# Latent attention on one core: its opening, four head-pair lists and the work between them written as one sequence

## The chip, the cores and the metric

The kernel runs on one core of one Trainium2 chip. A core has a matrix engine (TensorE, PE in the profile), three engines for elementwise work (VectorE or DVE, ScalarE or ACT, GpSimd or POOL), a queue engine (SyncE or SP) that mostly starts DMAs, and 16 DMA engines. [...] The metric is the device time in microseconds (us) of one execution: 1699.26 us before the change, the median of 3 runs (1699.22 to 1700.66).

## What is computed

One layer of a hybrid encoder step, on 1024 prompt tokens and 32 sample tokens with a cache of 512. All of it is float32; a product is formed from three matmuls over high and low parts of both operands. The change concerns branch A, the multi-head latent attention of the prompt (8 heads, taken in four pairs), and what is computed beside it.

```python
p = h @ w_in
q_lat, c_kv, k_r, q_b, k_b, v_b, g_a, g_b = jnp.split(p, IN_SPLITS, axis=-1)
q = (rms_norm(q_lat, g_q_lat) @ w_uq).reshape(B, T, H_A, NOPE + ROPE)
k_nope, v_a = expand_latent(c_kv, w_uk, w_uv)
s = (jnp.einsum('bqhd,bshd->bhqs', q_nope, k_nope)
     + jnp.einsum('bqhr,bsr->bhqs', q_rope, k_rope)).astype(jnp.float32) * MLA_SCALE
mask = (kpos[None, :] // CHUNK) <= (qpos[:, None] // CHUNK)
p = jax.nn.softmax(jnp.where(mask, s, NEG), axis=-1)
o_a = jnp.einsum('bhqs,bshd->bqhd', p.astype(v.dtype), v)
merged = g_a * (o_a @ w_proj_a) + g_b * (o_b @ w_proj_b)
```

## The kernel before

The stages run one after the other: input norm, combined projection, stick-breaking attention (branch B), latent vectors (`stage_lat`), latent attention (`stage_mla`), merge, ConvFFN. `stage_mla` is the one that changes.

Its heads go in four pairs p = 0 to 3. For each pair a *list* of tokens is written out by hand. A token names a pair, an action and a tile of the score matrix, and every token issues its instructions at once; inside a `manual_schedule` block TensorE, ScalarE and VectorE get them in exactly that order. SP and POOL (the DMAs) are not in the block; they go as soon as their queue and semaphores let them. The actions:

- `S` scores of a 128-row block (three matmuls of 256 to 512 columns and a mask of 64), `M`, `n`, `m` the negative maximum (VectorE), `E` the exponential with its sum (ScalarE), `s`, `R` sum and reciprocal, `C` or `c` the division (VectorE or ScalarE).
- `T` turn the probabilities (TensorE), `h` and `v` split them into high (ScalarE) and low (VectorE), `V` multiply by the value rows, `o` and `p` gather the two halves of the result.
- fill of the same list: `D` starts the next pair's expansion, `I` and `i` split its weights, `x` queries, `y` keys, `z` and `B` rotary parts, `X` and `K` query evacuation, `J` and `j` query splits, `H`, `g`, `L`, `b` key splits, `Z` the sample's queries, `Y` steps of the sample's own attention, `N` and `k` loads.
- fill shared by all: the output projection of branch B (`proj_b`). `U` loads weights, `W` and `w` split them, `f` is one step of three 264-column matmuls, `G` evacuates and stores a block. Its moving operand comes from DRAM in two halves of four tiles and is split into `ObH` (ScalarE) and `ObL` (VectorE).

Before the change there are three written orders. The *opening* is one string that expands pair 0, `zzzBBzzzBBzzzBByyHgLbyyHgLbxxxXKxxxXKxxxXK`, followed by the value blocks (`values`, four blocks of 12 matmuls, each followed by two evacuations on ScalarE and two on VectorE), the query splits, the rotary key rows, the first four operands (`O`), the store of the rotated keys (`krope_out`) and the first weight split. `ORDER_M` holds lists 0 and 1, `ORDER_N` lists 2 and 3. Between the two stand, in no written order, the sample's latent transposes (`mla_sample_latents`), the value blocks of the second half of the heads, the second half of the operands and four weight steps. Where one block ends and the next begins, the framework merges their instructions by its own estimate.

The lists overlap: list 1 begins while list 0 still turns its last probabilities. PSUM has eight banks: two each of the tags `mm` and `tr`, three of `s`, one of `pv`. The value rows of lists 2 and 3 take the two buffers of lists 0 and 1 (tag `V`), weights come through two buffers (`wr`), and of tag `big`, which holds query tiles and the operands' second half, there are three.

Lines in the profile are often a helper's: L68 is `hi` (a high part on ScalarE), L71 `lo` (a low part on VectorE), L75 to L77 the three matmuls of `mm3`, L806 the transposes of `T`, L820 the matmuls of `V`, L1615 to L1620 those of `S`, L954 to L959 the maxima, L961 the exponential, L1552 the value evacuation, L1830 the load of an operand, L1877 and L1878 `G`.

Of the kernel before, what the change touches and what calls it, by code (L numbers as in the profile page):

```python
# [17 lines left out]
P = 128  # L18
# [26 lines left out]
class K:  # L45
# [777 lines left out]
    def sb_weights(self, pieces, w):  # L823
# [27 lines left out]
        0S0.1 0M0.1 0n0.1 0S1.1 0E0.1 0S0.0 f4 W f 0M0.0 0n0.0 G 0M1.1 0n1.1 f2 w 0R0.1 0E1.1 f 0S1.0 0C0.1  # L851
        0M1.0 0E0.0 0S2.0b f2 0S2.0a f G 0R1.1 0n1.0 0R0.0 0M2.0b 0c0.0 0E1.0 0T0.0 0C1.1 0M2.0a 0h0.0 0m2.0 f
        0E2.0a 0R1.0 f2 0D 0c1.0 0S2.1b 0v0.0 G 0M2.1b 0S2.1a 0M2.1a 0m2.1 f 0E2.0b 0V0.0 0E2.1a f 0S3.0b 0M3.0b
        f 0o0 0E2.1b 0T1.1 0S3.0a 0p0 0T1.0 0s2.1 f G 0h1.1 0S3.1a 0M3.0a 0h1.0 0R2.1 0m3.0 f 0v1.1 0C2.1 f
        0s2.0 0M3.1a 0E3.0b f2 0S3.1b 0E3.0a G 0R2.0 0v1.0 f2 0c2.0 0M3.1b 0V1.1 0I 0V1.0 0S4.0b 0m3.1 0T2.1
        0E3.1a 0T2.2 0h2.2 0S4.0a 0i G 0M4.0b 0z 0M4.0a 0o1 0z 0m4.0 0E3.1b 0s3.0 0E4.0a 0v2.2 0z 0z 0z 0R3.0
        0s3.1 0T2.0 0h2.1 0B 0S4.1b 0h2.0 0B 0p1 0S4.1a 0V2.2 0E4.0b 0c3.0 0v2.1 0R3.1 W 0C3.1 0v2.0 0V2.1 0z
        0T3.2 0s4.0 0h3.2 0z 0M4.1a 0S5.0b 0M4.1b 0T3.3 0m4.1 0z 0E4.1b 0B 0M5.0b 0h3.3 0B 0V2.0 0S5.0a 0v3.3
        0o2 0M5.0a 0z 0B 0E4.1a 0m5.0 0x 0T3.1 0s4.1 0x 0B 0p2 0x 0R4.1 0v3.2 0S5.1b 0X 0V3.3 0E5.0b 0h3.1 0V3.2
        0v3.1 0E5.0a 0T3.0 0R4.0 0C4.1 0V3.1 0K 0h3.0 0c4.0 0v3.0 U 0S5.1a 0x 0M5.1b 0S6.1 0V3.0 0T4.3 0x 0o3 0x  # L860
        0M5.1a 0x 0s5.0 0m5.1 0T4.2 0h4.3 w 0M6.1 0v4.3 0x 0E5.1b 0X 0K 0p3 0h4.2 0R5.0 0T4.1 0h4.1 0n6.1 0x U
        0v4.2 0E5.1a 0E6.1 0V4.3 0s5.1 0c5.0 0X 0K 0V4.2 0T4.0 0S6.0 0v4.1 0R5.1 0h4.0 f 0C5.1 0J 0v4.0 f 0M6.0
        0S7.0 0n6.0 f 0V4.1 0T5.1 0T5.2 0M7.0 0V4.0 f 0h5.1 0j 0h5.2 G 0y 0v5.2 f 0E6.0 0R6.1 0y 0n7.0 0o4 f
        0R6.0 0H f 0E7.0 f 0T5.0 0p4 0C6.1 0c6.0 0L 0S7.1 0h5.0 0v5.1 0M7.1 0v5.0 0V5.2 0g 1S1.1 W 0T6.1 G 0n7.1
        0V5.1 0h6.1 0R7.0 1M1.1 0b 1n1.1 0E7.1 0V5.0 0y 0o5 0T6.0 1E1.1 0c7.0 0v6.1 0h6.0 1S0.0 0p5 w 0y 1S1.0
        1M0.0 f 0R7.1 0C7.1 0g 0V6.1 f 0H f 0T7.0 1S0.1 0v6.0 0V6.0 W 1n0.0 f 0b 1E0.0 1S2.0b 1M1.0 0L 1R0.0
        1n1.0 f w 1M0.1 1n0.1 1c0.0 0h7.0 1M2.0b 1E1.0 0o6 f 0v7.0 0p6 1S2.0a 1E0.1 1M2.0a f 1R0.1 f 1R1.0 1m2.0
        0J 1C0.1 1S2.1b 0V7.0 G G 0j 1R1.1 f 1M2.1b f 1T0.0 0o7 1E2.0b f 1C1.1 1S2.1a 1D U 1M2.1a 1E2.0a 1S3.0a
        1m2.1 f2 1c1.0 1h0.0 W 0p7 f 1s2.0 1E2.1a 1T1.0 1E2.1b 1M3.0a 1S3.0b 1S3.1b 1v0.0 w 1M3.0b G 1V0.0 1m3.0
        1s2.1 1R2.0 1T1.1 1h1.0 1o0 f 1R2.1 f 1E3.0a 1h1.1 G f 1M3.1b 1p0 1S3.1a 1E3.0b f 1c2.0 1v1.0 1k f 1v1.1  # L870
        1M3.1a 1s3.0 1m3.1 1C2.1 1V1.1 1V1.0 1S4.0a 1T2.2 f 1E3.1a 1o1 1E3.1b 1p1 1S4.0b 1T2.1 1M4.0a f 1h2.2
        1s3.1 G 1R3.0 1R3.1 f 1v2.2 1h2.1 1c3.0 1S4.1b 1M4.0b f 1v2.1 1T2.0 1m4.0 1C3.1 1V2.2 f 1E4.0a 1h2.0
        1S4.1a 1T3.3 1M4.1b 0Z 1v2.0 1I 1V2.1 1V2.0 1M4.1a 1E4.0b 1m4.1 1h3.3 1v3.3 1E4.1b 1o2 1i 1s4.0 1T3.2
        1E4.1a 1S5.0a 1S5.0b 1T3.1 1x 1h3.2 1S5.1b 1p2 1R4.0 1M5.0b G 1s4.1 1R4.1 1N 1c4.0 1x 1V3.3 1M5.0a 1m5.0
# [12 lines left out]
        f 0n1.0 0h0.0 0E1.0 0s2.0 0v0.0 0M2.1b 0R1.0 0M2.1a 0m2.1 0c1.0 0V0.0 0C1.1 G 0S3.0a 0M3.0a f2 0E2.1b
        0E2.1a 0T1.0 0S3.0b 0o0 0T1.1 f 0s2.1 0M3.0b 0h1.1 f 0m3.0 0R2.1 0R2.0 0p0 f 0h1.0 0E3.0b 0v1.1 0S3.1a f
        0S3.1b 0C2.1 f 0M3.1a 0c2.0 0M3.1b 0v1.0 0E3.0a f 0s3.0 G 0T2.0 0h2.0 0m3.1 0S4.0a 0E3.1a 0E3.1b 0v2.0 G
        f 0V1.1 0S4.0b 0T2.2 0M4.0a 0h2.2 f 0V1.0 0M4.0b 0T2.1 0m4.0 0o1 0h2.1 f 0p1 0s3.1 f 0S4.1a 0R3.0 f G  # L890
        0R3.1 0E4.0b f 0C3.1 0v2.1 0E4.0a 0v2.2 0c3.0 0M4.1a 0s4.0 0S5.0a 0S4.1b 0M4.1b f2 0V2.2 0T3.3 0m4.1 0I
        0M5.0a 0E4.1a 0V2.1 0T3.2 0h3.3 0i 0S5.0b 0V2.0 0v3.3 0M5.0b 0h3.2 G 0E4.1b 0x 0m5.0 0x 0v3.2 0T3.1 0o2
        0s4.1 0h3.1 0p2 0S5.1b 0R4.0 0x 0V3.3 U 0R4.1 0V3.2 0E5.0a 0c4.0 0v3.1 0T3.0 0C4.1 0S5.1a 0h3.0 0M5.1b
        0X 0M5.1a 0m5.1 0v3.0 0x 0T4.3 0E5.0b W 0E5.1b 0S6.0 0x 0h4.3 0M6.0 w 0n6.0 0v4.3 0E5.1a 0s5.0 0x 0K
        0V3.1 0V3.0 0T4.2 0X 0x 0s5.1 0R5.0 0T4.1 0o3 0p3 U 0x 0h4.2 0E6.0 0h4.1 0V4.3 0R5.1 0x 0v4.2 0K 0R6.0
        0V4.2 0T4.0 0C5.1 0v4.1 0S7.1 0S6.1 0X 0Z 0K 0h4.0 0c5.0 0V4.1 0T5.2 0Z 0J 0v4.0 f 0h5.2 f 0V4.0 f 0M7.1
        0n7.1 f 0M6.1 0E7.1 0j 0o4 0R7.1 0n6.1 0T5.1 G 0y 0p4 0y 0C7.1 0h5.1 0v5.2 0E6.1 0H 0v5.1 0R6.1 0C6.1
        0T5.0 f 0S7.0 0V5.2 0L 0h5.0 0J 1S0.0 0c6.0 f3 0T6.1 0M7.0 0g 0v5.0 0n7.0 0V5.1 0V5.0 0T6.0 1M0.0 0j 0b
        G 1S0.1 1n0.0 W 0h6.1 0E7.0 w 0R7.0 0o5 f 0c7.0 0v6.1 1M0.1 0y 0y f2 0h6.0 0p5 1n0.1 f 0V6.1 1S1.0 0T7.0
        1E0.1 W 0v6.0 1E0.0 1S2.0b 1S1.1 G 0h7.0 0V6.0 f 0H f2 0g f 1Y 1M1.0 1R0.1 0v7.0 1n1.0 1M1.1 1R0.0 1E1.0  # L900
        1c0.0 0o6 1Y 0L 1C0.1 1n1.1 1S2.0a 1R1.0 0p6 0V7.0 w 1E1.1 G 1Y 1M2.0b 1T0.0 1R1.1 1Y 0o7 1S2.1b f
        1M2.0a 1Y 1m2.0 1h0.0 1E2.0b 1c1.0 0p7 1M2.1b 1C1.1 1E2.0a 1v0.0 U 1S2.1a 1M2.1a 1s2.0 1V0.0 f 1Y 1T1.1
        1o0 1Y 1m2.1 1E2.1b 0b 1p0 1h1.1 1v1.1 1E2.1a 1s2.1 1T1.0 1R2.1 1h1.0 1R2.0 1C2.1 1Y 1V1.1 1v1.0 1c2.0
        1T2.1 1S3.0a 1h2.1 1T2.2 f 1Y 1V1.0 1v2.1 1Y f 1S3.0b 1T2.0 1M3.0a f 1Y f 1M3.0b 1m3.0 1h2.2 1o1 1S3.1a
        1v2.2 W 1q 1p1 1E3.0a 1E3.0b 1S3.1b 1Y 1M3.1a 1S4.0b 1V2.2 G 1M3.1b 1Y 1s3.0 1m3.1 1M4.0b 1Y 1V2.1
        1E3.1b 1Y 1R3.0 1S4.0a 1r 1h2.0 1v2.0 1E3.1a 1Y 1s3.1 1R3.1 1q 1M4.0a w 1C3.1 1c3.0 1Y 1m4.0 1S4.1b
        1T3.3 1E4.0a 1h3.3 1Y 1E4.0b 1M4.1b 1v3.3 1Y 1S4.1a 1V2.0 1T3.1 1Y 1M4.1a 1s4.0 1m4.1 1h3.1 1E4.1a 1o2
        1v3.1 1r 1T3.2 1p2 1Y 1V3.3 1h3.2 1v3.2 1V3.2 1T3.0 1E4.1b f 1V3.1 1s4.1 1R4.0 1R4.1 1c4.0 1h3.0 1S5.0a
        1Y 1Y 1C4.1 1v3.0 1T4.1 1T4.3 f 1M5.0a 1Y 1h4.3 1v4.3 1V3.0 1h4.1 1o3 1S5.1b G 1v4.1 1S5.0b 1T4.2 1M5.0b
        1Y 1m5.0 f 1q f 1p3 1h4.2 1V4.3 1E5.0b 1v4.2 1Y 1V4.2 1E5.0a 1r 1M5.1b 1T4.0 1S5.1a 1Y 1h4.0 1Y 1s5.0  # L910
# [1799 lines left out]
```

## Time and profile before

| | us |
|---|---|
| median of 3 runs | 1699.26 |
| profiled execution | 1700.54 |
| its span, first to last instruction | 1698.8 |
| latent attention, first opening matmul to last list row | about 573 to 840 |

| engine | busy, us | share of the span |
|---|---|---|
| PE (matmul) | 1647.6 | 97% |
| PEld (weight loads) | 1511.4 | 89% |
| DVE | 1269.9 | 75% |
| ACT | 1008.5 | 59% |
| POOL | 300.3 | 18% |

Two kinds of rows need a word. A row of a stretch gives its bounds, its length, and the busy time of PE, PEld, DVE, ACT and POOL in it with the number of instructions in brackets; then the clock that TensorE was granted (1.00 is full), the busy share of the DMA engines and GB/s. A row of the timeline gives start, length, engine, line, operation, tiles out<-in, shape and count, and in square brackets how long the engine sat idle before it and what it waited for. Neighbouring equal instructions are merged into one row. Matmuls overlap, so their lengths add up to more than the time they take; the step from one start to the next is what one of them costs.

### The profile page before, as it was taken

To read this page: it belongs to the slowest core of one execution; us is meant where nothing else is said; L and a number is where in the kernel's file an instruction comes from. 1 tells how busy PE (TensorE), PEld (TensorE's weight loads), DVE (VectorE), ACT (ScalarE), POOL (GpSimd) and SP (SyncE) were. 2 spreads that over 40 slices of the span, in tenths; PEclk is the share of its full clock that TensorE was granted. 3 is DMA by queue.
4 is the path that set the end of the run, shared out by engine and by line. 5 is a ranking of instruction groups with operands and counts; after the bars stand their busy time and mean duration, and the time that the engine had idled before them with its cause. 6 is when DMAs were issued, how large, how long until landed. Compare 5 with 4: busy or idle time off the path is not lost. (4 is left out here: it accounts for less than half of the span.)

```text
span 1698.8 us, 30285 instructions
## 1 busy us (share of the span) xinstructions
PE 1647.6 (97%) x11592; PEld 1511.4 (89%) x11592; DVE 1269.9 (75%) x2140; ACT 1008.5 (59%) x1945; POOL 300.3 (18%) x581
## 2 busy tenths in 40 slices
PE   5999999999999989999899999999999999999997
PEld 2899999999998879888788789999999999877885
DVE  4865698988873678888666789887777877787455
ACT  4544697978874568887763475444444444554442
POOL 5113312111110221111000212211111222200013
PEclk8999999999999989999999999999999999999999
DMA  9336885576532523321373532433333333697643
GB/s 358 103 109 198 277 244 163 164 194 182 169 111 56 163 79 96 96 62 60 110 250 127 181 124 77 150 107 133 127 104 131 131 104 121 240 321 246 205 139 121
DMA packets 194146, 260.62 MB, mean 153 GB/s; under 512 B 23375, under 2 KB 132305, under 8 KB 193937
## 3 DMA queue, kind: packets, MB, share of 16 engines
q1 hardware_dynamic: 172944, 198.50, 37.5%
q0 software_dynamic: 20688, 59.56, 9.9%
q8 instruction: 91, 1.49, 0.4%
q10 hardware_dynamic: 368, 0.63, 0.1%
q14 instruction: 55, 0.44, 0.1%
HBM read 191.11 MB, written 67.82 MB: 152 GB/s over the span
## 5 line engine op out<-in xcount | busy, mean ns | idle before, releaser
L68 ACT ACTIVATE wh<-wr 128x1024 fp32r<-128x1024 f32 (+2 forms) x151 | 130.2, 864 | 228.7 <-PE s L2164 85.8
L71 DVE TENSOR_TENSOR wl<-wr,wh 128x1024 fp32r<-128x1024 f32 (+2 forms) x151 | 148.3, 985 | 79.4 <-ACT wh L68 79.0
L75 PE MATMUL mm<-hh,wh 128*128 128x352 f32 x456 | 152.5, 334 | 0.1
L76 PE MATMUL mm<-hl,wh 128*128 128x352 f32 x456 | 148.5, 326 | 0.1
L77 PE MATMUL mm<-hh,wl 128*128 128x352 f32 x456 | 148.3, 325 | 0.0
L2163 PE MATMUL mm<-T,wh 128*128 128x256 f32 (+1 forms) x376 | 108.1, 288 | 0.0
L2165 PE MATMUL mm<-T,wl 128*128 128x256 f32 (+1 forms) x376 | 107.1, 285 | 0.4 <-DVE wl L71 0.2
L2164 PE MATMUL mm<-T,wh 128*128 128x256 f32 (+1 forms) x376 | 106.6, 284 | 0.0
L2165 PE MATMUL s<-T,wl 128*128 128x256 f32 (+1 forms) x348 | 99.3, 285 | 0.0
L2163 PE MATMUL s<-T,wh 128*128 128x256 f32 (+1 forms) x348 | 99.2, 285 | 0.0
L2164 PE MATMUL s<-T,wh 128*128 128x256 f32 (+1 forms) x348 | 98.8, 284 | 0.0
L71 DVE TENSOR_TENSOR wl<-S,wh 128x1024 fp32r<-128x1024 f32 (+1 forms) x55 | 59.1, 1077 | 51.0 <-ACT wh L68 50.7
L75 PEld LDWEIGHTS mm<-hh,wh 128*128 128x128 f32 x456 | 86.4, 189 | 3.7 <-issue 2.1
L2304 DVE SCALAR_TENSOR_TENSOR u<-u,c,u 128x1058 f32<-128x1058 f32 x68 | 87.0, 1317 | 2.0 <-ACT u L2301 0.7
L76 PEld LDWEIGHTS mm<-hl,wh 128*128 128x128 f32 x456 | 86.4, 189 | 2.2 <-DVE hl L333 0.7
L806 PE MATMUL tr<-c,A 128*128 128x128 f32 x576 | 87.2, 273 | 0.6 <-DVE ptd L71 0.6
L77 PEld LDWEIGHTS mm<-hh,wl 128*128 128x128 f32 x456 | 86.3, 189 | 0.6 <-issue 0.4
L68 ACT ACTIVATE wh<-S 128x1024 fp32r<-128x1024 f32 (+1 forms) x55 | 51.8, 943 | 48.0 <-PE s L2164 13.4
L2163 PE MATMUL tr<-T,wh 128*128 128x272 f32 (+1 forms) x272 | 77.8, 286 | 0.0
L2165 PE MATMUL tr<-T,wl 128*128 128x272 f32 (+1 forms) x272 | 77.6, 285 | 0.0
L2164 PE MATMUL tr<-T,wh 128*128 128x272 f32 (+1 forms) x272 | 77.3, 284 | 0.0
L71 DVE TENSOR_TENSOR PTl<-tr,PTh 128x512 fp32r<-128x512 f32 x96 | 65.3, 685 | 12.0 <-ACT PTh L68 11.3
(768 smaller groups left out, 5810.5 us busy)
## 6 DMA issues: line engine op xcount, KB each, us to landing
wr<-in_w_up_dram SPq DMA_DIRECT2D x44, 512.0 KB, 4.0
dr<-in_w_down_dram SPq DMA_DIRECT2D x43, 512.0 KB, 5.3
wr<-in_w_in_dram SPq DMA_DIRECT2D x33, 512.0 KB, 6.8
A<-in_w_ada_dram SPq DMA_DIRECT2D x32, 512.0 KB, 6.0
wr<-gdn SPq DMA_DIRECT2D x30, 512.0 KB, 4.7
gdn<-u POOLq DMA_DIRECT2D x23, 512.0 KB, 5.1
gd<-nat POOLq DMA_DIRECT2D x48, 176.0 KB, 3.6
t<-gd SPq DMA_DIRECT2D x16, 528.0 KB, 5.1
```

The source lines that it names most:

```text
L68: self.nc.scalar.activation(out, in_, AF.Identity, scale=scale)
L71: return self.nc.vector.tensor_tensor(out, full, hi.bitcast(F32), ALU.subtract)
L75: m(ps, lh, rh, start=start, stop=False)
L76: m(ps, lh, rl, start=False, stop=False)
L77: self.pe = m(ps, ll, rh, start=False, stop=stop).ins
L806: self.nc.tensor.transpose(tr[:, (2 * s + q) * P : (2 * s + q + 1) * P], at[q][:, b * P : b * P + P], self.idt)
L2163: m(ps[:, :n], w[0][:, k], x[0][:, k, c], start=first and k == 0, stop=False, skip_group_check=True)
L2164: m(ps[:, :n], w[0][:, k], x[1][:, k, c], start=False, stop=False, skip_group_check=True)
L2165: i = m(ps[:, :n], w[1][:, k], x[0][:, k, c], start=False, stop=k == 3, skip_group_check=True)
L2304: nc.vector.scalar_tensor_tensor(y, u[:, w : w + YW], self.cvT[:, w, cc : cc + 1], y, ALU.mult, ALU.add)
```

## The change

The opening, the four lists and what stands between them become one `ORDER_M`, in one `manual_schedule` block. Pairs are written 0 to 3; the digit 9 marks actions of the opening, 8 those of the value rows of the second half. New shared tokens: `Q` loads one operand, `e` and `l` make its high and low part, `a` is one step of the sample's latents. The value rows come apart into `S`, `s` (weight split), `A` (one block of matmuls), `c` (high part of one half of a block, ScalarE) and `d` (low part, VectorE). `krope_out` becomes a generator with steps `t` and `n`; `R` and `r` split the rotary key rows. The diff, cut (the order's untouched parts, from `0R4.1` to `1E5.1a` and from `2V2.0` to the end, read as before but for the pair's digit):

```diff
     ORDER_M = """
-        0S0.1 0M0.1 0n0.1 0S1.1 0E0.1 0S0.0 f4 W f 0M0.0 0n0.0 G 0M1.1 0n1.1 f2 w 0R0.1 0E1.1 f 0S1.0 0C0.1
...
+        9A 9z 9z 9z 9c 9d 9z 9z 9B 9z 9B 9z 9z 9c 9B 9B 9z 9y 9B 9y 9H 9x 9x 9B 9g 9x 9X 9K 9d 9A 9R 9c 9x 9c 9x
+        9r 9y Q 9x 9L 9x 9X 9d 9b 9y 9g 9H Q 9x 9x 9d 9A 9X 9b 9A 9J 9c 9K 9c 9L Q W 9j 9d 0S1.0 9d w 9K 9c Q e
+        0M1.0 e l e 0n1.0 0E1.0 l 0S0.0 0M0.0 e 0S1.1 f 9c l 9t 0n0.0 0E0.0 f 9d l 9d 0R0.0 0S2.0a f W 0c0.0
+        0S0.1 f G f 0M0.1 0R1.0 f 0n0.1 0E0.1 f2 w 0R0.1 0c1.0 0M1.1 G 9n 0S2.0b 0C0.1 0n1.1 0M2.0b 0E1.1 f
...
+        2M0.1 1n7.1 l 1T6.0 1h6.1 2n0.1 1y 1o5 1p5 1v6.1 1y 1E7.1 1h6.0 1v6.0 1R7.1 2S0.0 2E0.1 1C7.1 8S 1V6.1
+        1H 1V6.0 8s a 2S2.0b 1o6 2M0.0 a 2n0.0 G 1T7.0 1h7.0 1p6 1L 2S1.0 8A 2M2.0b 2R0.1 2M1.0 1g 2E0.0 2n1.0
+        2S2.0a 1v7.0 e 2C0.1 8c 1V7.0 a 2E1.0 8d 1o7 2M2.0a 2m2.0 2S1.1 8c 1b 2R0.0 2D 2E2.0b a 8d 2M1.1 8A Q
+        2c0.0 w 2n1.1 2E2.0a 2T0.0 e 2S2.1a l 2M2.1a 2E1.1 2h0.0 8c 2S2.1b 2M2.1b 2R1.0 2m2.1 8c 2v0.0 2s2.0
+        2R1.1 8d 2C1.1 2E2.1b 8A 2c1.0 f 2S3.0b 2E2.1a 2S3.0a 2T1.0 f 1p7 8d l 2M3.0a Q 2h1.0 8A f e 8c 2v1.0 l
...
     """.split()
-    def mla_attend(self, order, lists):
+    def mla_attend(self, lists, others, shared):
...
+            if p is None or p in others:
+                for _ in range(int(x or 1)):
+                    (shared if p is None else others[p])(k)
+                continue
...
-            for k in "zzzBBzzzBBzzzBByyHgLbyyHgLbxxxXKxxxXKxxxXK":
-                steps[k]()
-            next(vstep)
-            for k in "JjJj":
-                steps[k]()
...
-        for b, order in enumerate((self.ORDER_M, self.ORDER_N)):
-            if b:
-                self.mla_sample_latents()
-                Vs, vstep = values(1, raws[1], "mm tr")
-                list(vstep)
-                proj["U"]()
-                list(proj["O"]())
-                for k in "UWwU":
-                    proj[k]()
-            with self.tc.manual_schedule(engines={E.PE, E.Activation, E.DVE}):
-                self.mla_attend(order, [lambda p=p, v=Vs: one(p, v) for p in (2 * b, 2 * b + 1)])
+        with self.tc.manual_schedule(engines={E.PE, E.Activation, E.DVE}):
+            self.mla_attend({p: lambda p=p: one(p) for p in range(4)}, {8: second, 9: lambda k: first[k]()}, shared)
...
+        def operand(i):
+            k = done[3 + i] % 4
+            done[3 + i] += 1
+            if i:
+                self.lo(obs[-1][1][:, k], fs.pop(0), obs[-1][0][:, k])
+            else:
+                if not k:
+                    obs.append([self.tl(M, [P, 4, HC], F32R, g) for g in ("ObH", "ObL")])
+                self.hi(obs[-1][0][:, k], fs[done[3] - 1 - done[4]])
```

Same instructions of the three engines are issued before and after; their order differs, and with it the order in which SP and POOL are handed their DMAs.

More of the change, by code (lines that the diff above doesn't have):

```diff
@@ L929, in mla_attend @@
             score, fill, tiles, banks, stats, common = ctx[p]
-            k, x = x[0], x[1:]
             if k not in "SMmnEsRCcThvVop":
-                for _ in range(int(x or 1)):
-                    fill(k)
+                fill(k)
                 continue
@@ L1404, in out @@
             nc.gpsimd.dma_start(ks[2 * P - w3 :], st[:w, 352:384])
-        self.krope_out = out
+            yield
+        self.krope_out = out()
         lp.release()
@@ L1555, in values, with high, low, block @@
-            return Vs, steps()
+            gt, ps, done = cycle(gt.split()), [], [0, 0]
+            def high():
+                self.hi(w[0][:, :512], raw[:, :512])
+            def low():
+                self.lo(w[1][:, :512], raw[:, :512], w[0][:, :512])
+            def block():
+                x, t, (h, l) = self.bank(next(gt)), 2 * len(ps), w
+                for j in range(2):
+                    tk = slice((t + j) * P, (t + j + 1) * P)
+                    for k in range(2):
+                        self.mm3(x[:, j * 256 : j * 256 + 256], self.CPh[k][:, tk], self.CPl[k][:, tk],
+                                 h[:, k * 256 : k * 256 + 256], l[:, k * 256 : k * 256 + 256], k == 0, k == 1)
+                ps.append(x.rearrange("r (j q h d) -> r j q h d", j=2, q=2, h=2))
@@ L1558, in stage_mla, with part @@
+            def part(i):
+                t, q = divmod(done[i], 2)
+                done[i] += 1
+                v = Vs[q][:, 2 * t : 2 * t + 2]
+                if i:
+                    self.lo(v[:, :, :, 64:128], ps[t][:, :, q], v[:, :, :, 0:64])
+                else:
+                    nc.scalar.activation(v[:, :, :, 0:64], ps[t][:, :, q], AF.Identity)
+            return Vs, dict(S=high, s=low, A=block, c=lambda: part(0), d=lambda: part(1))
         AB = [[self.tl(self.W, [P, 1024], F32R, g) for g in ("wh", "wl")] for _ in range(2)]
@@ L1628, in fill @@
             def fill(k):
[L1629 to L1631 removed]
+                if k == "D":
                     expand(p)
@@ L1644, in fill, with second, shared @@
                     nexts[p][k]()
-            return score, lambda b, h: Vs[p % 2][:, b, h], out, fill
-        for b, order in enumerate((self.ORDER_M, self.ORDER_N)):
-            if b:
-                self.mla_sample_latents()
-                Vs, vstep = values(1, raws[1], "mm tr")
-                list(vstep)
-                proj["U"]()
-                list(proj["O"]())
-                for k in "UWwU":
-                    proj[k]()
-            with self.tc.manual_schedule(engines={E.PE, E.Activation, E.DVE}):
-                self.mla_attend(order, [lambda p=p, v=Vs: one(p, v) for p in (2 * b, 2 * b + 1)])
+            return score, lambda b, h: Vs[p // 2][p % 2][:, b, h], out, fill
+        Vs, later, latents = {0: V0}, {}, []
+        def second(k):
+            if not later:
+                Vs[1], x = values(1, raws[1], "mm tr")
+                later.update(x)
+            later[k]()
+        def shared(k):
+            if k != "a":
+                return proj[k]()
+            if not latents:
+                latents.append(self.mla_sample_latents())
+            next(latents[0])
+        E = mybir.EngineType
+        with self.tc.manual_schedule(engines={E.PE, E.Activation, E.DVE}):
+            self.mla_attend({p: lambda p=p: one(p) for p in range(4)}, {8: second, 9: lambda k: first[k]()}, shared)
         for _ in split(self.osm[:, 3], slice(0, P), slice(TP, T)):
@@ L1696, in mla_sample_latents @@
         nc.vector.tensor_copy(KSm[:, :, PAST:], new)
+        yield
         for k in range(2):
@@ L1880, in proj_b @@
         step = steps()
-        return dict(P=fetch, O=operands, U=load, W=high, w=low, f=lambda: next(step), G=store)
+        return dict(Q=fetch, e=lambda: operand(0), l=lambda: operand(1), U=load, W=high, w=low, f=lambda: next(step), G=store)
     def natural(self, facc, lhs, ws, first, done=None, sample=None, tiles=range(8)):
```

202 lines of the change are left out of this document (86 added, 116 removed).

## The prediction

> **What bounds the kernel now.** I read the page first, then the stretches of the attention stage, then five-microsecond slices of its two bad places, and last the instructions in order of time there. The first two lines are the page's.
>
> ```profile
> span 1698.8 us, 30285 instructions
> PE 1647.6 (97%) x11592; PEld 1511.4 (89%) x11592; DVE 1269.9 (75%) x2140; ACT 1008.5 (59%) x1945; POOL 300.3 (18%) x581
> ```
>
> TensorE holds the time: 51 us of its span are idle. The change edits the latent attention alone. Matching the score tokens of the two written lists to the score matmuls, one by one, puts it from 573 to 840 us, and it also shows what the change leaves alone. The new list is word for word the old one from the middle of list 0 (`0R4.1`) to the end of list 1 (`1E5.1a`), 342 instructions' worth of tokens, and from the middle of list 2 (`2V2.0`) to the end of list 3, 480 more. Those are the stretches 636 to 694 and 749 to 840. What is rewritten is two seams: the opening with the first half of list 0, 573 to 636, and the last quarter of list 1 with the first half of list 2, 694 to 749. Each row below gives a stretch's length and the busy time of each engine in it; the clock stands after POOL.
>
> ```profile
> 573.00:636.00 63.00, 54.94 (x355) 50.32 (x348) 44.04 (x105) 36.93 (x84) 15.52 (x31) 0.89 0.37 104
> 636.00:694.00 58.00, 58.00 (x425) 53.59 (x424) 51.79 (x135) 50.25 (x118) 9.23 (x17) 1.00 0.31 93
> 694.00:749.00 55.00, 52.05 (x374) 47.77 (x373) 44.58 (x111) 43.91 (x102) 8.21 (x14) 0.97 0.30 86
> 749.00:840.00 91.00, 89.67 (x641) 79.80 (x640) 72.97 (x191) 74.38 (x177) 9.77 (x18) 1.00 0.19 57
> ```
>
> The stretch 636 to 694 is what this code does when its order is good: PE never idle, weight loads 53.59 of 58 (92%), VectorE 89%, ScalarE 87%. The seams have 80% and 87% of weight loads, at a clock below 1. The slices show where:
>
> ```profile
> 590.00:595.00 5.00, 2.37 (x17) 1.77 (x15) 4.78 (x9) 3.20 (x7) 1.05 (x2) 1.00 0.66 151
> 595.00:600.00 5.00, 1.79 (x8) 1.24 (x6) 3.70 (x10) 3.11 (x8) 0.00 (x0) 0.52 0.01 2
> 600.00:605.00 5.00, 2.78 (x11) 2.47 (x12) 3.40 (x10) 1.07 (x4) 4.31 (x7) 0.50 0.42 107
> 605.00:610.00 5.00, 5.00 (x27) 4.69 (x27) 0.76 (x5) 1.97 (x6) 1.14 (x3) 0.62 0.50 108
> 720.00:725.00 5.00, 2.19 (x16) 1.82 (x15) 4.20 (x15) 3.15 (x9) 0.00 (x0) 0.99 0.27 105
> 725.00:730.00 5.00, 5.00 (x26) 4.61 (x25) 2.94 (x8) 3.18 (x10) 0.57 (x1) 0.67 0.22 58
> ```
>
> and the instructions name the releasers, in square brackets behind the idle time:
>
> ```profile
> 592.52 0.39 PE L1616 MATMUL s<-KL,QH 128*128 128x256 f32 x1 [1.22 <-DVE KL L71]
> 594.56 0.47 PE L1615 MATMUL s<-KH,QH 128*128 128x512 f32 x1 [1.41 <-DVE mx L959]
> 601.13 0.59 PE L75 MATMUL mm<-ObH,wh 128*128 128x264 f32 x1 [4.34 <-ACT wh L68]
> 603.03 0.59 PE L77 MATMUL mm<-ObH,wl 128*128 128x264 f32 x1 [1.09 <-DVE wl L71]
> 723.60 0.42 PE L1615 MATMUL s<-KH,QH 128*128 128x320 f32 x1 [2.81 <-ACT A L961]
> ```
>
> The 4.34 us are an ordering loss and no lack of work. The weights of the first output-projection step (512 columns, token `W` of the opening) are split by
>
> ```profile
> 595.19 1.06 ACT L68 ACTIVATE wh<-wr 128x1024 fp32r<-128x1024 f32 x1
> 599.18 1.22 DVE L71 TENSOR_TENSOR wl<-wr,wh 128x1024 fp32r<-128x1024 f32 x1
> 600.45 0.62 ACT L68 ACTIVATE wh<-wr 128x512 fp32r<-128x512 f32 x1
> 602.28 0.69 DVE L71 TENSOR_TENSOR wl<-wr,wh 128x512 fp32r<-128x512 f32 x1
> ```
>
> The 1024-wide split belongs to the second weight set, which is the first list's, and it ran ahead of the opening's 512-wide one. So opening and list, each in a written order of its own, were shuffled together, and the piece PE needs first came last.
>
> **The change part by part.** No instruction of the three engines appears or goes: the counts of every token kind agree (128 `f`, 96 `S`, 16 value parts `c` and `d` each, 12 `W`). The work of the seams is therefore fixed and only its order is priced.
>
> *What is lost now.* Opening: 1.22 + 1.41 + 4.34 + 1.09 = 8.06 us idle. Then the low clock: 1.79, 2.78 and 5.00 us of busy PE at 0.52, 0.50 and 0.62 cost 0.86 + 1.39 + 1.90 = 4.15. Together 12.2. Middle: 2.81 idle and 5.00 x 0.33 = 1.65 of clock, together 4.5. Sum 16.7.
>
> *What the new order keeps of it, opening.* The value blocks now stand among the rotary and key steps, not after them; the first score still waits for the same chain: rotary products, the rotated rows out to DRAM and back, the query splits.
>
> ```profile
> 584.99 0.28 PE L75 MATMUL mm<-wh,lat 128*128 128x256 f32 x1
> ...
> 590.57 0.28 PE L77 MATMUL mm<-wh,lat 128*128 128x256 f32 x1
> ...
> 580.20 0.53 SPq L1478 DMA_DIRECT2D rqc<-VSm  x1
> 587.77 2.00 ACT L68 ACTIVATE QH<-big 128x1024 fp32r<-128x1024 f32 x2
> 588.85 2.36 DVE L71 TENSOR_TENSOR QL<-big,QH 128x1024 fp32r<-128x1024 f32 x2 [0.52 <-ACT QH L68]
> 585.96 1.79 SPq L1830 DMA_DIRECT2D A<-ob  x4
> ```
>
> The rows leave at 580.20 because SP is busy until then; the four value blocks' 48 matmuls, first and last shown, took 5.7 us, so the one block that now stands ahead (12) puts the last rotary product about 1.4 us later and the write some 0.5 us later. So `J`, the query split, begins near 588.5 as now, and with one pair split ahead of the first score instead of two (the second `J` and `j` now come in the list), that score ends near 592, the first exponential near 594.5. PE has nothing to do in about 1 of the 1.5 us before that score's low part. Then come the operand splits `e`, `l`, whose prices are
>
> ```profile
> L1552 ACT ACTIVATE V<-mm 128x256 fp32r<-128x256 f32 x8 | 3.1, 384 | 3.8 <-DVE V L71 3.4 <-PE mm L77 0.4
> L71 DVE TENSOR_TENSOR V<-mm,V 128x256 fp32r<-128x256 f32 x8 | 3.3, 418 | 2.3 <-ACT V L1552 2.2
> L68 ACT ACTIVATE ObH<-A 128x528 fp32r<-128x528 f32 x4 | 2.6, 641 | 0.0
> L71 DVE TENSOR_TENSOR ObL<-A,ObH 128x528 fp32r<-128x528 f32 x4 | 2.8, 702 | 0.1
> A<-ob SPq DMA_DIRECT2D x4, 264.0 KB, 4.5
> 703.20 0.28 PE L75 MATMUL mm<-ObH,wh 128*128 128x264 f32 x1
> 703.32 0.28 PE L76 MATMUL mm<-ObL,wh 128*128 128x264 f32 x1
> ```
>
> The loads `Q` follow the query rows on SP (585.96 now) and land 4.5 us later, so the first `e` can run near 592. The first `f` then waits for `w` (0.69) and one `l` (0.70) behind it, near 594.4; the next three are spaced by one `l` each, 0.70 us against 3 x 0.12 = 0.36 for the three matmuls of an `f` (the last two rows' starts), with two scores and the three transposes of `t` standing between them. That is another 2 us of idle, 3.0 in all. The clock: now 2.63 us of idle in the first two gaps were enough for 0.52; the new gaps are of that size. Bounds for what stays of the 12.2: nothing from below; from above both first gaps and the whole clock loss, 2.63 + 4.15 = 6.8. I take 3.0 idle + 1.5 clock = 4.5, nearer the upper end, because the chain in front of the first score is not shortened. Opening: -7.7 (-5.4 to -12.2).
>
> [...]
>
> *Middle.* Latent transposes `a`, value blocks `8A` with their parts, and operand splits are spread from the end of list 1 over the first half of list 2, where before they ran in a lump between two lists and the first maxima waited behind them. List 2's first scores start while list 1 still turns its probabilities, as lists 0 and 1 overlap already. Kept: at least nothing, at most all 4.5; I take 0.5, since in the untouched overlap of lists 0 and 1 no idle row stands at all (58.00 of 58.00). Middle: -4.0 (0 to -4.5).
>
> *Costed at nothing.* The added `yield`s and the unwinding of helpers issue nothing. The moved value and operand splits need room: with the seams at 55.3 and 51 us VectorE would be busy 80% and 87%, ScalarE 67% and 86%, below the 89% and 87% that 636 to 694 sustains with PE full; that is the cover, and in the middle it is nearly used up. Past it each 0.418 us of a value part is 0.418 us of PE. The third weight load `U` moves from the opening to the middle of list 0; SP runs ahead of the lists and is held only by the two weight buffers, so it lands before its `W`. The DRAM stores of the rotary keys (`n`) keep their place on POOL among the stores of list 0.
>
> *New waits.* `R` (1.06 us on ScalarE) stands earlier and waits for the key rows' landing; behind it are two value parts and the query split, which waits for later rows anyway. `e` waits for a load, behind it are the first exponential and `f`'s store `G`. In the middle `Q` is written one at a time; four loads share three buffers, so the third is released by `l` of the first and the fourth by `l` of the second.
>
> **The sum.** 7.7 + 4.0 = 11.7 off the profiled execution's 1700.54 us (span 1698.8) is 1688.8; the runs' median is 1699.26, 1.3 lower, so by the median 1687.6. I predict 1688. The weight-load share checks it: at the 92.4% of 636 to 694 the seams would last 50.32/0.924 = 54.5 and 47.77/0.924 = 51.7, 11.8 less. [...]
>
> **The rivals.**
>
> *More comes of it.* If VectorE alone bounds the seams and holds 89.3%, they last 49.3 and 49.9, 18.8 us less: 1681. For it: nothing else is near its limit. Against it: the opening's DRAM round trip, which no order shortens.
>
> *The opening gives nothing, or the order isn't lived.* `f` steps done early are missing as fill later; the first half of list 0 then idles where it is now covered, and only the middle's idle of 2.81 is won: 1697.7. For it: 24 `f` stand in that half before and after. Against it: PE's seam has 8 us of plain idle, and VectorE is at 70% there.
>
> *Slower: ScalarE stands before loads that SP holds.* The three engines follow the list to the letter, SP does not follow it, and it is strictly in order. Now SP holds operand loads until their buffer is free (from the start of the one to the end of the next pass 8.22 us), and ScalarE waits for one:
>
> ```profile
> 701.20 8.22 SPq L1830 DMA_DIRECT2D big<-ob  x2
> ACT ObH L68 <- DMA big<-ob: 2.2, 1, 2.2
> ```
>
> In the new list the fourth `Q` is four tokens ahead of its `e`. If such holds reach ScalarE, everything behind `e`, exponentials and turned probabilities, stops, and PE with them. If ScalarE had to sit out such a hold in full, one of 8.22 us eats 70% of the gain, two make 16.4 - 11.7 = 4.7 us slower: 1705. It decides from 11.7 us of holds on. Against it: `l` of the second operand, the releaser, stands some 30 tokens ahead of the fourth `e`, about 6 us by the pace of list 2, more than the 4.5 us of a landing.
>
> **How the numbers follow.** Forecast 0.62 (own range, from the two parts' bounds: 1684 to 1695), more 0.14, nothing from the opening 0.10, slower 0.14. A measurement of this kernel tells about 0.2%, 3.4 us, from no change. Faster: 0.62 + 0.14 and 0.03 of the third case, 0.79; same 0.07; slower 0.14. The range of 1681 to 1702 takes in the first three cases and leaves out most of the fourth and the far edge of the second.
>
> **What would show it.** Right: the first output-projection matmul (264 columns) at about 594 instead of 601; no idle row over 2 us from 590 to 610; PEclk back at 1.00 before 605; no 2.81 us gap at the start of list 2, its value parts between exponentials; the unchanged 58 us and 91 us stretches as long as before. Wrong: a ScalarE row waiting for an operand load for more than 3 us, a VectorE share above 90% with idle PE in the middle seam, or untouched stretches that grow.

## The result and the profile after

The changed kernel takes 1691.26 us (median of 4 runs, 1688.20 to 1692.11), the kernel before, run beside it, 1699.96 us (4 runs, 1699.22 to 1701.65): ratio 0.9944, 95% interval 0.9927 to 0.9961. It is 8.7 us faster; 11.7 were forecast, and 1691.26 lies inside the stated range. Its profiled execution took 1692.0 us.

First the page of the changed kernel: span and busy times.

```profile
span 1690.2 us, 30269 instructions
PE 1647.4 (97%) x11592; PEld 1511.3 (89%) x11592; DVE 1268.7 (75%) x2140; ACT 1007.4 (60%) x1945; POOL 299.2 (18%) x581
```

The work is the same to the instruction on TensorE, VectorE and ScalarE. What went is idle TensorE time: 51.2 us of the span before, 42.8 now. Matching the score matmuls one by one again gives the four stretches in the times of the new trace, with the columns as before.

```profile
573.00:631.00 58.00, 53.36 (x354) 48.67 (x348) 42.84 (x105) 36.57 (x82) 15.98 (x31) 0.97 0.42 103
631.00:689.00 58.00, 58.00 (x425) 53.58 (x425) 51.72 (x134) 51.29 (x119) 8.78 (x16) 1.00 0.34 100
689.00:739.00 50.00, 49.97 (x373) 46.02 (x372) 44.38 (x112) 42.93 (x102) 7.99 (x14) 1.00 0.28 82
739.00:830.00 91.00, 89.70 (x641) 79.88 (x640) 73.39 (x192) 74.31 (x177) 9.82 (x18) 1.00 0.21 64
```

The two copied stretches last 58 and 91 us as before. The middle seam fell from 55 to 50 us and has nothing left to give: PE 49.97 of 50.00 at a clock of 1.00. The opening seam fell from 63 to 58 and still holds 4.64 us of idle PE. Slices of five microseconds of the changed kernel show where:

```profile
590.00:595.00 5.00, 4.84 (x37) 4.03 (x35) 4.52 (x8) 4.43 (x9) 0.00 (x0) 1.00 0.93 167
595.00:600.00 5.00, 4.59 (x33) 3.96 (x33) 4.76 (x14) 4.90 (x14) 0.17 (x1) 1.00 0.53 105
600.00:605.00 5.00, 3.14 (x26) 2.93 (x24) 2.27 (x7) 2.06 (x7) 1.39 (x3) 1.00 0.37 110
605.00:610.00 5.00, 4.76 (x22) 4.48 (x22) 3.75 (x10) 4.32 (x13) 4.43 (x8) 0.66 0.16 28
```

The ten microseconds from 590 had 4.16 us of busy TensorE before and have 9.43 now. A new hole stands behind them, in which VectorE and ScalarE have little to do too (busy 2.27 and 2.06 of 5.00): all three wait for something else. The timeline of the changed kernel names it.

```profile
594.92 0.36 PE L75 MATMUL mm<-ObH,wh 128*128 128x264 f32 x1
599.83 0.58 POOL L1890 DMA_DIRECT2D pbd<-nat  x1 [12.13 <-ACT nat L1889]
601.27 0.55 POOL L1890 DMA_DIRECT2D pbd<-nat  x1 [0.87 <-ACT nat L1889]
603.91 0.37 ACT L1397 COPY nat<-tr 128x256 f32<-128x256 f32 x1 [2.94 <-DMA pbd<-nat]
604.33 0.77 ACT L962 ACTIVATE A<-s,mx,lat 128x512 f32<-128x512 f32 x1
604.57 2.11 POOL L1401 DMA_DIRECT2D out_dram<-nat  x3 [2.75 <-ACT nat L1398]
605.24 0.44 PE L1619 MATMUL s<-KH,QH 128*128 128x384 f32 x1 [2.10 <-ACT A L962]
```

The row to read is the fourth. `n` copies the rotary keys into a staging tile of the kind `nat`, of which there are two. Both hold blocks of the output projection (`G`, L1889) on their way to DRAM, so the copy waits for the first of these stores, issued at 599.83, to land. Behind the copy on ScalarE stands an exponential (L962) for which TensorE waits. In the kernel before, the same copy stood 5.6 us ahead of the first `G`, its stores stood ahead of that block's store on POOL's queue, and nobody waited for a tile:

```profile
600.04 0.36 ACT L1395 COPY nat<-tr 128x256 f32<-128x256 f32 x1
600.69 2.15 POOL L1399 DMA_DIRECT2D out_dram<-nat  x3 [7.42 <-ACT nat L1396]
...
605.63 0.38 ACT L1877 COPY nat<-mm 128x264 f32<-128x264 f32 x1 [4.56 <-PE mm L77]
606.31 0.57 POOL L1878 DMA_DIRECT2D pbd<-nat  x1 [1.29 <-ACT nat L1877]
```

The 8.5 us by which the trace's span is shorter are read from the shift of matching matmuls: -4.95 at the end of the opening seam, a further -4.98 over the middle one, which makes -9.99 at the last score of list 3, then +2.36 at the start of the merge and -0.9 over the later stages. The merge is not touched; its first gap is about as long as before (2.79 us, 2.67 before), but the clock behind it fell to 0.50 where it had stayed at 1.00 (the last section sets more such gaps side by side). Gap and slice, before and then after:

```profile
845.19 0.59 PE L75 MATMUL mm<-KH,wh 128*128 128x352 f32 x2 [2.67 <-ACT KH L68]
845.00:850.00 5.00, 4.59 (x27) 4.30 (x28) 3.65 (x3) 3.15 (x4) 0.36 (x7) 1.00 1.04 421
```

```profile
835.29 0.96 PE L75 MATMUL mm<-KH,wh 128*128 128x352 f32 x2 [2.79 <-ACT KH L68]
835.00:840.00 5.00, 4.71 (x16) 4.71 (x17) 3.65 (x3) 3.25 (x4) 0.46 (x8) 0.50 1.02 413
```

### The profile page after: what moved, and what is told of

Same layout as the page of the kernel before. It is cut to its first block, busy times and chain, and to the rows that moved or that the text cites. A ratio compares the mean times of both kernels' runs of the same rounds, so it can differ in the third digit from the quotient of the medians.

```text
span 1690.2 us, 30269 instructions
## 1 busy us (share of the span) xinstructions
PE 1647.4 (97%) x11592; PEld 1511.3 (89%) x11592; DVE 1268.7 (75%) x2140; ACT 1007.4 (60%) x1945; POOL 299.2 (18%) x581
```

## The experiments

**The two seams apart.** Theory: two independent gains, the opening's cut short by the wait of `n`. The rival: the gains hang together, one seam alone gives nothing. The first kernel has the new opening, and then lists 2 and 3 with their lump between them in the old order; the second the old opening and the new order from the middle of list 0 on.

```diff
# h1_open_new: the new sequence ends with list 1
+        for _ in "aaaaaaa":
+            shared("a")
...
+        with self.tc.manual_schedule(engines={E.PE, E.Activation, E.DVE}):
+            self.mla_attend(..., self.ORDER_N)
# h2_middle_new: the opening's calls as before, the sequence begins with list 0's old first half
+            for k in "zzzBBzzzBBzzzByyHgLbyyHgLbxxxXKxxxXKxxxXKAcdcdJjJjRr":
+                first[k]()
```

> New opening and new first half of list 0, then the old list 1, the old unwritten work between lists 1 and 2, and the old second order. Theory (each seam wins by itself, and each win is kept to the end of the stage): the last score of list 3 comes about 5.0 us earlier than before, all of it ahead of list 0's 5.1b score, and the 2.8 us gap at the start of list 2 is there again; about 0.3% faster. Rival (the opening's win needs the new middle, for instance because fill done early is missing later): the shift shrinks below 3 us by the end of list 3.

> Old opening with its own block and old first half of list 0, then the new end of list 1 and first half of list 2. Theory: nothing shifts before the end of list 1, the 4.3 us gap at the first projection step is back, and list 2 from 5.1b on comes about 5.0 us earlier; about 0.3% faster. Rival: the middle's win is in part the opening's, under 3 us by itself.

Measured: the opening alone 1695.65 us, ratio 0.9973 (0.9963 to 0.9982); the middle alone 1693.1, ratio 0.996 (0.9948 to 0.9973); the kernel before beside them 1700.1. Both gain, and each where it was changed: list 0's score `5.1b` is earlier by 5.9 us in the first (counted from the opening's start, as in the table below) and by nothing in the second; list 2's `5.1b` by 0.1 us more in the first and by 4.6 in the second. So each gain comes without the other. (The medians alone would not say it so well: 4.5 and 7.0 us apart, 8.7 together.) The first shows the wait again, 3.20 us at `n` and 2.37 us of idle TensorE behind it, but its clock stays at 1.00, which fits the 1.1 us that it gains beyond the same opening in the changed kernel.

**The wait of `n`: its tile or its place.** The copy gets a tile of another kind, or its old tile at an earlier place, ahead of the first `G`.

```diff
# e1_own_tile
-            st, w = self.tl(self.At, [P, 512], F32, "nat"), TQ - 2 * P
+            st, w = self.tl(self.At, [P, 512], F32R, "PTh").bitcast(F32), TQ - 2 * P
# e2_n_early
-        ... 0n0.0 0E0.0 f 9d l 9d 0R0.0 0S2.0a f W 0c0.0 0S0.1 f G ... 0M1.1 G 9n 0S2.0b
+        ... 0n0.0 0E0.0 f 9d l 9d 0R0.0 0S2.0a 9n f W 0c0.0 0S0.1 f G ... 0M1.1 G 0S2.0b
```

> The changed kernel, but the rotated keys are staged for their store in a PTh buffer instead of a nat buffer, so that step n no longer waits for a projection store to land. Theory (the opening fell short because of this one wait): ScalarE's 2.94 us wait at 601 and PE's 2.10 us gap behind it go, the clock stays at 1.00 from 605 to 610, and list 0's 5.1b score comes 2.5 to 3.7 us earlier than in the changed kernel; the whole kernel 2 to 4 us faster than the changed one. Rival (the wait only moves: POOL's seven stores hold the next projection blocks, or VectorE is the next bound): under 1 us.

> The changed kernel with token n written before the first G instead of behind the second. Theory: the wait for a landed store goes for n, but the seven key stores now stand on POOL ahead of the first projection stores, so the second or third G waits for its buffer instead; win over the changed kernel 1 to 3.5 us. Rival (that order was as good as any): no change within 0.5 us, with a wait of about 3 us at a G.

Measured: the tile of its own 1686.52 us, ratio 0.9922 (0.9909 to 0.9935); the earlier place 1692.58, ratio 0.9953 (0.9941 to 0.9966). The first is 4.7 us below the changed kernel, more than the 2 to 4 expected; 3.9 of them are in the opening, and its trace loses nothing at the start of the merge either. The second wins nothing: 1.3 us above the changed kernel. With the tile of its own the slice that held 3.14 us of TensorE is full, at full clock:

```profile
600.00:605.00 5.00, 5.00 (x39) 4.81 (x38) 4.26 (x13) 4.80 (x14) 4.14 (x7) 1.00 0.47 130
```

With the earlier place the copy itself waits for nothing, and a `G` behind it now waits for the key rows' stores:

```profile
605.23 0.38 ACT L1882 COPY nat<-mm 128x264 f32<-128x264 f32 x1 [4.26 <-DMA out_dram<-nat]
605.66 0.59 PE L75 MATMUL mm<-ObH,wh 128*128 128x264 f32 x1 [2.62 <-ACT nat L1882]
```

Three users within 6 us and two tiles: in all these orders the third stands for the landing of the first. The two places tried for `n` only choose who that is; a third place to stage removes the wait. It cost 2.10 us of idle and, at 0.66 of the clock, 4.76 x 0.34 = 1.6 more, together 3.7 of the 3.9 us that the tile of its own wins in the opening. The 1.6 us are not fixed: the new opening alone had the longer gap, 2.37 us, and lost no clock.

**Was the old 4.34 us gap an ordering loss?** Twice the kernel before with the opening's 512-column split `W`, `w` moved up: ahead of the first operand split, and then, as that put it among the value blocks, ahead of the operand splits but behind the value blocks. The second edit so moves two things: the operand splits, which stood among the value blocks, now follow them too. In the first of these the split writes the buffer that still holds the value weights, so three of the four value blocks of pairs 0 and 1 are multiplied with the projection's weights.

```diff
# e3_split_first
+            proj["W"]()
+            proj["w"]()
             ob = proj["O"]()
             next(ob)
             for _ in vstep:
                 next(ob)
...
-            proj["W"]()
-            proj["w"]()
# e9_split_after_values
-            ob = proj["O"]()
-            next(ob)
-            for _ in vstep:
-                next(ob)
+            list(vstep)
+            proj["W"]()
+            proj["w"]()
+            ob = proj["O"]()
+            for _ in range(4):
+                next(ob)
```

> The kernel before, with one thing moved: the opening's own weight split (`W`, `w`, 512 columns) is written ahead of the three operand splits of the opening instead of behind them. It asks whether the 4.34 us gap of the kernel before was only an order in which the 512-column split came last. If that is all of it, the gap falls to what the operand splits leave, 1 to 2 us, the clock of 595 to 605 stays near 0.5 to 0.8, and the time falls by 2 to 5 us, to about 1695 to 1698. If the split was late because the queues of VectorE and ScalarE were full of the first list's maxima and exponentials anyway, the gap stays over 3 us and the time within 1.5 us of the kernel before.

> The kernel before, with the opening's weight split (`W`, `w`) and then the four operand splits written behind the last value block, which read the buffer that the split writes. The first list's tokens are shuffled in by the scheduler as before. If the 4.34 us gap of the kernel before was only that this split came behind the list's wider one, the gap goes, the first output-projection matmul comes 3 us earlier, and the time falls by 2 to 4 us, to about 1696. If something else stands next in line, the first output-projection matmul comes earlier all the same, but a wait for a `nat` buffer of over 2 us opens within the ten microseconds behind it, and the last score of list 0's first half stays within 1 us of where it is: 1699.

Measured: the first 1703.36 us, ratio 1.002 (1.001 to 1.003): the value blocks stood 4.96 us for that split, a wait of the edit's own making, so on the gap it answers nothing. It shows the two tiles once more, in the old order: with the first `G` only 1.9 us behind `n`, at 603.03, the second stands 4.14 us for the key rows' store. The second kernel takes 1698.22, ratio 0.9991 (0.9982 to 1.000), with these waits where the kernel before had 4.34 and 1.09:

```profile
598.04 0.59 PE L75 MATMUL mm<-ObH,wh 128*128 128x264 f32 x1 [1.45 <-ACT ObH L68]
600.51 0.59 PE L76 MATMUL mm<-ObL,wh 128*128 128x264 f32 x1 [1.89 <-DVE ObL L71]
```

The first output-projection matmul comes 3.1 us earlier and list 0's first half ends 2.8 us earlier, while no wait for a `nat` buffer opens. So the order there did lose time: the split's place, with the operand splits moved along, is worth 2.8 of the 12.2 us that the prediction counted as lost in the opening, and the operand splits, four in a row, are next in line. Of the two expectations neither came whole: the first matmul came earlier as both said, no `nat` wait opened, and the whole time is 1698.22 where 1696 or 1699 stood. Most of the 2.8 us is not seen in it: 0.6 go in the middle gap, 3.43 us instead of 2.81, and 1.5 at the start of the merge.

**What else holds the opening.** In the changed kernel ScalarE stands 2.33 us at `K` (L1496), the copy of a query block into a `big` tile that the store of the rotary rows still reads; `R`, the high part of the key rows, stands behind it on ScalarE, and its low part behind that on VectorE. Behind that low part stand the low parts of value rows, and for one of these TensorE waits 1.96 us (the fourth row). (The expectations call this `K` a key block's split and `R` a scaling; they are the query block's copy and the key rows' high part.)

```profile
584.09 0.46 ACT L1496 ACTIVATE big<-s 64x352 f32<-64x352 f32 x1 [2.33 <-DMA rqs<-big]
584.58 1.06 ACT L68 ACTIVATE KH<-A 64x1024 fp32r<-64x1024 f32 x1
585.66 1.22 DVE L71 TENSOR_TENSOR KL<-A,KH 64x1024 fp32r<-64x1024 f32 x1 [2.80 <-ACT KH L68]
...
589.65 0.36 PE L75 MATMUL s<-wh,lat 128*128 128x256 f32 x1 [1.96 <-DVE V L71]
...
595.80 0.66 ACT L962 ACTIVATE A<-s,mx,lat 128x384 f32<-128x384 f32 x1
```

One kernel moves `R` ahead of `K`, one has that and the tile of its own.

```diff
# e5_R_first, e6_both
-        ... 9y 9H 9x 9x 9B 9g 9x 9X 9K 9d 9A 9R 9c 9x 9c 9x
+        ... 9y 9H 9x 9x 9B 9g 9x 9X 9R 9K 9d 9A 9c 9x 9c 9x
```

> The changed kernel, with the scaling of the new rotary rows (`9R`) written ahead of the third key block's split (`9K`) instead of behind it; in the changed kernel that split stands 2.33 us at the rotary store and pushes `R` and VectorE behind it. If the chain to the first score bounds the opening, its first exponential comes up to 1.2 us earlier and so does everything from list 0 on: about 1690. If the wait of `n` for its buffer sets when list 0 gets going, the earlier exponentials only stand longer at it: the wait grows from 2.9 to about 4 us and the time stays within 1 us of 1691.

> The changed kernel with both edits: `n` staged in a tile of its own kind, and `R` ahead of the third key block's split. If the two waits follow each other on the path, with the buffer's wait gone the earlier `R` shows, 0.5 to 1.2 us below the kernel with the tile of its own alone (1686.5): about 1685.5. If `R` was covered by the loads that the operand splits wait for, the two kernels agree within 0.5 us.

Measured: 1686.99 us, ratio 0.9925 (0.9913 to 0.9938), and with both 1685.61, ratio 0.9922 (0.9909 to 0.9936). The first is a miss for both theories: the exponential came 0.9 us earlier (594.92 for 595.80) as the one said, but the wait of `n` shrank, where the other had it grow, and the kernel is 4.3 us faster than the changed one where 1 was the most expected. The rows of that kernel:

```profile
594.92 0.66 ACT L955 ACTIVATE A<-s,mx,lat 128x384 f32<-128x384 f32 x1
...
598.96 0.58 POOL L1883 DMA_DIRECT2D pbd<-nat  x1 [13.57 <-ACT nat L1882]
601.21 0.37 ACT L1390 COPY nat<-tr 128x256 f32<-128x256 f32 x1 [1.13 <-DMA pbd<-nat]
```

From the store's issue to the copy it is 2.25 us here and 4.08 in the changed kernel, for the same 132 KB. From 585 to 610 no PE gap is over 0.4 us: the 1.96 us wait for the value rows is gone, as in all three kernels that move `R` and in none of the other five with the new opening, and the 2.10 us behind `n` is gone too; the clock stays at 1.00. The sooner landing is not `R`'s doing as far as the traces tell: that store took 4.3 us to land in the kernel with both edits and 2.3 in the one with all three, and their openings are the same. What sets it is open, and how much of the -9.1 us of this kernel's opening is luck with it. With both edits the opening gains 2.1 us more than with the tile alone, where the value rows still cost 2.15 us at that place; that part is `R`'s.

**The gap at the start of the merge.** Twelve matmuls that nobody reads go into it, in the changed kernel and in the one with both edits.

```diff
+        ps = self.bank("pv")
+        h, l, _ = self.pa[0]
+        for _ in range(4):
+            self.mm3(ps[:, :352], h[:, 1], l[:, 1], self.xh[1][:, :352], self.xl[1][:, :352], True, True)
```

> The changed kernel with twelve matmuls more, 352 columns each, whose result nobody reads: they repeat a product of the output projection and stand on TensorE in the gap of 2.79 us at the start of the merge (835.29), where it waits for the first list's rows. At 0.155 us each, as the rows around them are spaced, they take 1.9 us of it. If the 0.50 and 0.82 of granted clock behind that gap are what the changed kernel gives back there, the clock stays at 1.00, and the time falls by 2 to 3 us, to about 1689, though the kernel does more work. If the clock falls there for another reason (the load of the stage, transfers), the time stays at 1691 or rises by up to 1 us.

> All three edits together: `n` staged in a tile of its own kind, `R` ahead of the third key block's split, and the twelve matmuls in the gap at the start of the merge, where the kernel with the first two alone shows 0.66 in one slice of five microseconds (about 1.7 us of work lost). By the clock's theory 1 to 2 us below that kernel's 1685.6: about 1684. If the gap does not matter: 1685.6 or up to 1 us more.

Measured: 1691.52 us (1686.74 to 1695.14), ratio 0.9954 (0.9939 to 0.9969), and 1685.39, ratio 0.9919 (0.9906 to 0.9932). The changed kernel with the filler:

```profile
834.91 0.59 PE L75 MATMUL mm<-KH,wh 128*128 128x352 f32 x2 [0.78 <-ACT KH L68]
835.00:840.00 5.00, 4.78 (x28) 4.49 (x29) 3.54 (x3) 3.13 (x3) 0.47 (x8) 1.00 1.02 415
```

The clock stays at 1.00 and the stage gives nothing back, as the clock's theory said, yet the medians do not move, as the other said. In the first kernel's trace, its slowest run, the shift stands at -10.3 us from the merge on, where the changed kernel has -7.6; it then loses 1.6 us around 1064 and 3.1 around 1528, where TensorE waits for weight splits of later stages that no edit touches:

```profile
1064.50 0.38 PE L2182 MATMUL tr<-T,wl 128*128 128x256 f32 x1 [1.19 <-DVE wl L71]
1527.71 1.22 PE L2518 MATMUL mm<-d,wl 128*128 128x512 f32 x2 [2.12 <-DVE wl L71]
```

So the price of the gap is seen in the stage and not in the whole time. And two traces without the filler, the kernel before and the tile of its own alone, lost nothing there either, so the filler is one way out of that loss and not the only one.

All ten kernels and the changed one, by the shift of matching instructions against the kernel before, in us: over the opening (from its first mask row, near 573, to list 0's score `5.1b`), over the middle (to list 2's `5.1b`), and over the start of the merge (from list 3's last score to 860 in the time of before), with the length of the gap there. Each kernel has one trace; where the gap is 2.49 us or more, the column of the merge goes with the clock granted there, which the last section gives for eight of the traces.

| kernel | median | opening | middle | merge start | gap |
|---|---|---|---|---|---|
| before | 1698.8 to 1700.1 | 0 | 0 | 0 | 2.67 |
| changed | 1691.26 | -4.8 | -5.0 | +2.4 | 2.79 |
| new opening alone | 1695.65 | -5.9 | -0.1 | +1.5 | 2.61 |
| new middle alone | 1693.1 | 0.0 | -4.6 | +1.0 | 2.57 |
| `n` with its own tile | 1686.52 | -8.6 | -4.6 | -0.1 | 2.54 |
| `n` earlier | 1692.58 | -4.5 | -4.9 | +1.4 | 2.52 |
| `R` first | 1686.99 | -9.1 | -4.6 | +0.7 | 2.49 |
| own tile and `R` first | 1685.61 | -10.8 | -5.0 | +1.5 | 2.62 |
| changed, gap filled | 1691.52 | -4.7 | -5.0 | 0.0 | 0.78 |
| all three | 1685.39 | -10.8 | -4.6 | -0.2 | 0.68 |
| split first | 1703.36 | +1.7 | -1.2 | +1.4 | 2.54 |
| split after the values | 1698.22 | -2.8 | +0.6 | +1.5 | 2.60 |

The four kernels with `n`'s own tile, `R` first, or both are faster than either kernel of the case. The best is some 1685.5 us, 14 below the kernel before; between 1685.61 and 1685.39 the runs do not tell.

## Why the prediction was right, and where it was off

- *What bounds, and the seams:* right. The two seams hold the gain, the copied stretches kept 58 and 91 us, and the seams gain independently.
- *Middle, -4.0 (0 to -4.5):* right in mechanism. -5.0 in the changed kernel, -4.6 to -5.0 in the kernels that have the new middle: no 2.81 us gap, 0.03 us of idle left where 0.5 were kept. That it passed the bound of -4.5 by up to 0.5 says that the loss before was a little under-counted: 2.95 us of the old seam were idle (52.05 of 55.00), 2.81 were counted.
- *Opening, -7.7 (-5.4 to -12.2):* direction right, the term mis-sized: -4.8, outside its own bounds. The first `f` came at 594.92 (forecast 594.4; before 601.13), and the clock stood at 1.00 up to 605, but "no idle row over 2 us from 590 to 610" did not hold: 2.10 us at 605.24, and 0.66 of the clock behind it. What was kept is not what was kept in the sum, either. Its 3.0 us of idle, around the first score and between the first `f` steps, are 0.57 in the slices from 590 to 600; in their place came 1.96 us at 589.65 and 2.10 at 605.24. Its 1.5 us of clock look met by 1.6, by luck: they were meant for those first gaps, where the clock stayed at 1.00, and went behind a wait that the sum did not have.
- *The step that failed* is the sentence among those costed at nothing: "The DRAM stores of the rotary keys (`n`) keep their place on POOL among the stores of list 0." They did not: before, they were issued from 600.69 on, ahead of the first `G`'s store at 606.31; now two `G` stores, at 599.83 and 601.27, stand ahead of them, at 604.57. Nor was the queue what cost the time. `n` also takes one of two `nat` tiles, and the new order puts it third, behind two `G`. The tile of its own shows the price: 3.9 us in the opening, with which it gives -8.6, inside the bounds and 0.9 past the forecast.
- *The chain in front of the first score "is not shortened":* the first `J` began at 589.96 where 588.5 was forecast, and the first exponential at 595.80 for 594.5. Part of that came from the order, as moving `R` shows (594.92, with both edits 594.49). The "New waits" had seen `R` behind the key rows, and two value parts behind `R`, at no price; that ScalarE would stand 2.33 us ahead of it, at `K`, and TensorE 1.96 us for those value rows, they had not.
- *The ordering loss behind the 4.34 us:* right in kind. Repairing that place in the old kernel, the operand splits moved along, gives 2.8 us in the opening.
- *The sum:* 7.7 + 4.0 = 11.7 against 4.95 + 4.98 = 9.9 by list 3's end; the merge's clock, 0.50 from 835 to 840, then took 2.4 back in this trace, for which the sum had no term, and the later stages gave 0.9. The trace's 8.5 is what stayed, near the median's 8.7. That 1691.26 came no nearer to 1688 is so in part the opening's mis-sized term and in part the clock at one gap of the merge. A small slip of the sums: the range of 1684 to 1695 and the rivals' 1697.7 and 1705 count from the profiled execution, the forecast from the median, 1.3 us lower.
- *The rivals:* none came. The wait that did appear is a cousin of the slower one: ScalarE in order before a DMA. But it was a store that held it, on POOL's queue, 2.94 us long and once; the price was worked out for loads held by SP.

## What to carry to other kernels

When steps are reordered by hand, list for each moved step the buffers that it takes beside the engine that runs it, and count who else takes a buffer of that kind within one DMA landing (here 2 to 4 us): the one too many stops its engine with everything behind it (here ScalarE for 2.94 us), and here trading places within that time only moved the wait. A short idle row can have a second price in the slice behind it, the granted clock (here 0.66 behind 2.10 us); read both. That price differed here from trace to trace, in a stage that no edit touched too (0 to 2.4 us at gaps of 2.49 to 2.79 us), so follow the shift of matching instructions stage by stage to the end of the trace, and do not put a change of the clock down to an edit before you have seen it in more than one trace.

## What the runs showed of the hardware

In these traces the length of an idle gap of TensorE did not by itself tell whether the granted clock fell. At the start of the merge, a stage that no edit but the filler touches, the same wait of 2.49 to 2.79 us stood in ten traces. The 30 us around it, in eight traces: with 2.67 us (before) and 2.54 (`n` with its own tile) the clock was 1.00 and nothing was lost; with 2.49 to 2.62 in five others (both seams apart, `n` earlier, `R` first, own tile and `R` first) it was 0.94 and 0.7 to 1.5 us went; with 2.79 (the changed kernel) it was 0.89 and 2.4 us went. The rows of the kernel before, of `n` with its own tile, of `n` earlier (2.52 us) and of the changed kernel, in this order:

```profile
828.00:858.00 30.00, 26.30 (x179) 24.86 (x178) 19.47 (x38) 18.90 (x36) 3.16 (x13) 1.00 0.45 165
828.00:858.00 30.00, 27.25 (x168) 23.27 (x167) 22.33 (x28) 18.70 (x23) 0.49 (x9) 1.00 0.83 308
828.00:858.00 30.00, 27.15 (x174) 24.07 (x173) 20.43 (x31) 15.83 (x21) 2.09 (x11) 0.94 0.69 253
828.00:858.00 30.00, 27.10 (x167) 24.40 (x166) 19.50 (x29) 15.55 (x21) 2.08 (x11) 0.89 0.68 251
```

So 2.54 us lost nothing and 2.52 us lost 1.4. With the gap filled to 0.78 or 0.68 nothing was lost in either trace.

The openings show the same. The clock was 1.00 in the slices from 590 to 600 behind a gap of 1.96 us in the changed kernel (ending at 589.65) and one of 2.15 with the tile of its own (589.61), and in those from 600 to 610 around the 2.37 us of the new opening alone (603.59). It was 0.66 from 605 to 610 with 2.10 us in the changed kernel (605.24) and 2.62 with `n` earlier (605.66). In the kernel before, two gaps of 1.22 and 1.41 us, which ended 2.0 us apart (592.52 and 594.56), were followed by 0.52 from 595 to 600.

What tells a gap that costs clock from one that does not, these runs do not show. The price of a gap of 2 to 3 us could not be read from its length. Nor can the 2.4 us at the merge be put down to the new order: `n` with its own tile has that order and lost nothing there, and the kernel with the split after the values has the old one and lost 1.5.
